# A table of steps for the work beside the output projection and the first two blocks of the MLP

## The chip, the cores and the metric

The kernel is one program on one core of one Trainium2 chip. TensorE (PE) does matrix products and transposes and writes to PSUM; VectorE (DVE) and ScalarE (ACT) do elementwise work, GpSimd (POOL) a little of it, SyncE (SP) and ACT issue transfers. Each engine runs its own queue in the order in which the program issued it, and waits at an instruction until what that instruction reads or overwrites is free. The metric is the time of one execution on the device, in microseconds, lower is better: 1658.2 is the median of 3 runs of the kernel before.

## The reference

One layer of a hybrid diffusion backbone on 1024 latent tokens and 128 context tokens (1152 rows, nine blocks t = 0..8 of 128) with 1024 channels. In float32:

```python
mod = (silu(cond) @ w_mod + b_mod)[:, None, :]
sh1, sc1, g1, sh2, sc2, g2 = split(mod, 6)
h = x * (1 + sc1) + sh1
q, k, v, u, bg, cg, ga, gc = split(h @ w_in, ...)
attn = merge_heads(attend(q, k, v)) @ w_attn_proj
conv = (bg * short_conv(cg * u, conv_w, conv_b)) @ w_conv_proj
mix = (sigmoid(ga) * attn + sigmoid(gc) * conv) @ w_o
x = layer_norm(ALPHA * x + g1 * mix, ln1_g, ln1_b)
h = x * (1 + sc2) + sh2
f = square(relu(h @ w1 + b1)) @ w2 + b2
x = layer_norm(ALPHA * x + g2 * f, ln2_g, ln2_b)
```

The case is about the stretch from `@ w_o` over the layer norm and `h = x * (1 + sc2) + sh2` to the beginning of `h @ w1`.

## The kernel before, in words

**Precision.** Every float32 operand is cut in a high part (a cast on ACT) and a low part (the rest, a subtraction on DVE), and a product is three matmuls: high by high, high by low, low by high.

**The output projection** has 18 units g = 0..17. A unit multiplies one block t of 128 tokens by one half (512) of the output channels: eight contraction steps kb of three matmuls (L1318, L1319, L1320), 24 in all, into one PSUM bank. The units run in three passes: half 0 of t0 to t5 (g0 to g5), half 1 of t0 to t8 (g6 to g14), half 0 of t6 to t8 (g15 to g17). In the last unit of a pass the weights of the next are split (L109 on ACT and L122 on DVE, L1257 and L1258 for some).

**Beside the projection.** After a unit, `ln1_sum` (L1047, L1048, L1051, all on DVE) adds the residual rows and takes statistics. Once both halves of a block are there, `ln1_apply` (with `moments`: DVE L1037, ACT's root L1038, DVE L1039 and L1040; then ACT L1059) normalizes the block. `turn` transposes a half of the block on PE (four transposes, L1113, to a bank) and writes it, scaled and shifted by the modulation, to the raw tiles, one column of 128 channels at a time, by ACT (L1126) or DVE (L1128). `n_vec` of the four columns are DVE's.

**The MLP's first layer** is a Winograd form of Strassen's scheme: 7 products instead of 8. The tokens are two pairs of 2 x 288 = 576 tokens. Pair 0 has t0 to t3 and the first half of t4, pair 1 the rest. Of a pair there are four raw tiles of 4 x 288 columns (`q00`, `q01`, `q10`, `q11`, holding B11, B12, B21, B22), with one buffer each, which both pairs use in turn. From them the sums T1 = B12 - B11, T3 = B22 - B12, T2 = B22 - T1 and T4 = B21 - T2 are made (`sub`, DVE L1151, over the raw tiles), and B11, T1, T2, B21, T3, B22, T4 are each cut in a high part (`high`, ACT L1140) and a low one (`low`, DVE L1147). A block multiplies one group of output channels by them in seven steps, in the order B11, B21, T1, T2, B22, T3, T4 (`ORDER`). The first two blocks are narrow: block 0 (steps 0 to 6) is for pair 0 alone and block 1 (steps 7 to 13) for pair 1 alone, so that block 0 can start before pair 1 is there. A step of theirs has 12 matmuls of 288 columns (L1388 to L1390), and after it ACT keeps the product (`keep`, L1451) or DVE adds it to a kept one (`plus`, L1454). All later blocks do both pairs; block 2's first product is written to a bank that the trace names dX. Weight sums (L826) and their splits (L1211 on ACT, L1212 on DVE) run some steps ahead, and ACT applies relu and square (L1396, L1397).

**What sets the order.** In the projection a queue `todo` holds pieces, each with a cost in microseconds that was written by hand; `spend(0.69)` after each kb of a unit adds credit and issues pieces from the front of the queue for as long as the credit is not negative. A unit's sum goes to the front, a turn to the end. In a pass's last unit nothing but one piece is issued. In the blocks, `beside` holds pieces by step of block 0, and `pair_parts(0..6)` issues the parts of pair 1 up to one step ahead of their use in block 1. The turns of t4 (second half), t5 and t6 for pair 1 are put at the queue's end and mostly run after the projection.

## Time and profile before

| | |
|---|---|
| median of 3 runs (lowest, highest) | 1658.2 us (1656.58, 1659.09) |
| the profiled execution: its time, its span | 1657.08 us, 1655.3 us |
| mean granted clock of PE in it | 0.986 |
| busy share of PE, DVE, ACT | 96%, 63%, 43% |
| projection and first two blocks in it, from g0 to the third block's first matmul | about 761.3 to 921.69 us |

A matmul's row in the trace begins where the previous one is well under way, so that the pitch of the starts and not the length of a row is what a matmul costs PE. Behind a row, in brackets, stands how long the engine had been idle and which instruction released it. In the table of waits a line reads: engine, tile and line of the waiting instruction, then what it waited for, then total, count and the longest in us. L numbers are lines of the kernel before; the changed kernel's lines are higher by some 5 to 40.

### The profile page before, as it was taken

What the parts mean: (1) busy time and instruction counts of PE and PEld (TensorE: products, weight loads), DVE (VectorE), ACT (ScalarE), POOL (GpSimd) and SP (SyncE); (2) the same over time, 40 slices, a digit from 0 to 9 for tenths busy, and PEclk for the clock granted to TensorE, in tenths of its full rate; (3) what the DMA queues carried; (4) which work ended last, traced back from release to release, by engine and by line L of the source; (5) the groups of instructions that cost most, each with busy time, mean ns of one, the idle gap of its engine ahead of it and who ended that gap; (6) DMA issues with size and microseconds to landing.
All of it is one profiled execution on the core that took longest, in us unless ns stands there. A gap on an engine that the chain in (4) does not pass through costs nothing.

```text
span 1655.3 us, 27274 instructions
## 1 busy us (share of the span) xinstructions
PE 1594.0 (96%) x10432; PEld 1536.8 (93%) x10432; DVE 1046.2 (63%) x1826; ACT 717.2 (43%) x1344; POOL 201.8 (12%) x214
## 2 busy tenths in 40 slices
PE   7999999999999999999988899999999999999995
PEld 5799999999999999998877899999999999999995
DVE  6568888665556553335577666666665558865666
ACT  5367777611112112222356556565565335453030
POOL 2145555100000002211000000000000121000002
PEclk9999999999999999999999999999999999999998
DMA  8432122142322323314333344554448898788792
GB/s 320 141 89 73 50 70 54 52 122 89 122 97 64 91 88 90 107 60 147 115 108 128 135 160 163 173 180 155 165 154 301 283 318 278 231 258 235 233 326 89
DMA packets 147563, 252.94 MB, mean 153 GB/s; under 512 B 40240, under 2 KB 58288, under 8 KB 147432
## 3 DMA queue, kind: packets, MB, share of 16 engines
q1 hardware_dynamic: 117064, 203.99, 39.0%
q10 hardware_dynamic: 30368, 47.20, 7.8%
q8 instruction: 82, 1.34, 0.3%
q14 instruction: 49, 0.40, 0.1%
HBM read 187.93 MB, written 63.21 MB: 152 GB/s over the span
## 4 chain that ended last, share of the span: by engine, by line
PE 79%; DVE 8%; ACT 5%; issue 3%; DMA 3%; POOL 1%; SPq 0%; POOLq 0%; ACTq 0%; DVEq 0%
PE ps L363 8%; PE ps L365 8%; PE ps L361 8%; PE pq L1641 6%; PE pq L1643 6%; PE pq L1642 6%; PE dX L1388 3%; PE dX L1390 3%; PE dX L1389 3%; PE dV L1388 2%; PE dV L1390 2%; PE dV L1389 2%; PE ps L882 2%; PE ps L883 2%; PE ps L881 2%
## 5 line engine op out<-in xcount | busy, mean ns | idle before, releaser
L365 PE MATMUL ps<-ahi,wl 128*128 128x384 f32 x864 | 292.6, 339 | 0.2 <-DVE wl L122 0.2
L363 PE MATMUL ps<-alo,wh 128*128 128x384 f32 x864 | 292.5, 338 | 0.0
L361 PE MATMUL ps<-ahi,wh 128*128 128x384 f32 x864 | 292.5, 338 | 0.0
L1641 PE MATMUL pq<-xh,vh 128*128 128x288 f32 x640 | 190.5, 298 | 4.7 <-ACT accc L1736 3.2
L1642 PE MATMUL pq<-xl,vh 128*128 128x288 f32 x640 | 189.6, 296 | 0.0
L1643 PE MATMUL pq<-xh,vl 128*128 128x288 f32 x640 | 189.0, 295 | 0.2 <-DVE vl L1631 0.2
L361 PEld LDWEIGHTS ps<-ahi,wh 128*128 128x128 f32 x864 | 162.4, 188 | 1.4 <-issue 0.2
L363 PEld LDWEIGHTS ps<-alo,wh 128*128 128x128 f32 x864 | 162.4, 188 | 0.7
L365 PEld LDWEIGHTS ps<-ahi,wl 128*128 128x128 f32 x864 | 162.4, 188 | 0.5 <-DVE wl L122 0.5
L1641 PEld LDWEIGHTS pq<-xh,vh 128*128 128x128 f32 x640 | 120.6, 188 | 5.6 <-ACT accc L1736 3.4
L1643 PEld LDWEIGHTS pq<-xh,vl 128*128 128x128 f32 x640 | 121.2, 189 | 0.4 <-DVE vl L1631 0.4
L1642 PEld LDWEIGHTS pq<-xl,vh 128*128 128x128 f32 x640 | 120.9, 189 | 0.1
L1608 DVE TENSOR_TENSOR xl<-hraw,xh 128x576 fp32r<-128x576 f32 x80 | 60.5, 756 | 74.5 <-ACT xh L1604 74.5
L122 DVE TENSOR_TENSOR wl<-wr,wh 128x1024 fp32r<-128x1024 f32 (+1 forms) x52 | 58.6, 1130 | 75.3 <-ACT wh L109 74.9
L1604 ACT CAST xh<-hraw 128x576 fp32r<-128x576 f32 x80 | 53.9, 673 | 96.4 <-issue 44.5
L1788 POOL TENSOR_TENSOR xm<-xm,ag 128x1024 f32<-128x1024 f32 x9 | 22.4, 2484 | 593.3 <-DMA w2r<-w 532.7
L743 DVE SCALAR_TENSOR_TENSOR acc<-wmb,sil,acc 128x512 f32<-128x512 f32 x112 | 78.2, 747 | 11.2 <-DMA wmb<-wmb 11.0
L109 ACT CAST wh<-wr 128x1024 fp32r<-128x1024 f32 (+1 forms) x60 | 55.9, 946 | 37.7 <-PE ps L1320 28.7
L563 ACT ACTIVATE s<-s,st 128x512 f32<-128x512 f32 (+1 forms) x72 | 49.6, 689 | 51.6 <-DVE st L561 51.1
L1451 ACT ACTIVATE c<-dX,b1c 128x576 f32<-128x576 f32 x45 | 33.3, 741 | 73.1 <-PE dX L1390 73.1
L882 PE MATMUL ps<-acl,wh 128*128 128x384 f32 x192 | 64.2, 334 | 0.0
L883 PE MATMUL ps<-ach,wl 128*128 128x384 f32 x192 | 64.2, 334 | 0.0
(378 smaller groups left out, 4388.6 us busy)
## 6 DMA issues: line engine op xcount, KB each, us to landing
w2r<-w SPq DMA_DIRECT2D x144, 256.0 KB
hraw<-hdT SPq DMA_DIRECT2D x60, 288.0 KB
wmb<-wmb SPq DMA_DIRECT2D x64, 256.0 KB
w1r<-w SPq DMA_DIRECT2D x30, 512.0 KB
hdB<-h ACTq DMA_DIRECT2D x48, 288.0 KB
hdT<-hT ACTq DMA_DIRECT2D x48, 288.0 KB
hraw<-hdB SPq DMA_DIRECT2D x44, 288.0 KB
mr<-wma SPq DMA_DIRECT2D x16, 512.0 KB
```

What stands on the lines that cost most here:

```text
L361: mm(b[:, :CH], lhsT=hi[:, ws], rhs=a[0][:, kb, :], start=first and kb == 0, stop=False)
L363: mm(b[:, :CH], lhsT=hi[:, ws], rhs=a[1][:, kb, :], start=False, stop=False)
L365: mm(b[:, :CH], lhsT=lo[:, ws], rhs=a[0][:, kb, :], start=False, stop=last and kb == n - 1)
L743: vec.scalar_tensor_tensor(out=a, in0=t, scalar=sil[:, k, cond:cond + 1], in1=a, op0=ALU.mult, op1=ALU.add)
L882: mm(b[:, :CH], lhsT=hi[:, ws], rhs=parts[kb][1][:, cs_], start=False, stop=False)
L883: mm(b[:, :CH], lhsT=lo[:, ws], rhs=parts[kb][0][:, cs_], start=False, stop=kb == 3)
L1388: mm(o, lhsT=hi[:, ws], rhs=xh, start=first and kb == 0, stop=False, **kw)
L1389: mm(o, lhsT=hi[:, ws], rhs=xl, start=False, stop=False, **kw)
L1390: mm(o, lhsT=lo[:, ws], rhs=xh, start=False, stop=kb == 3, **kw)
L1641: mm(o, lhsT=hi[:, ws], rhs=xh[:, i], start=j == 0, stop=False)
L1642: mm(o, lhsT=hi[:, ws], rhs=xl[:, i], start=False, stop=False)
L1643: mm(o, lhsT=lo[:, ws], rhs=xh[:, i], start=False, stop=j == NJ - 1)
```

## The change: what it does

1. *Projection by table.* The queue and its costs are gone. `at(g, kb, ...)` puts a piece into a slot of the table, after contraction step kb of unit g, and the loop issues what its slot holds. A unit's `ln1_sum` is issued after kb 0 of the next unit.
2. *Stages.* The layer norm is issued in two stages, `ln1_deviation` (statistics and root) after kb 1 and `ln1_apply` after kb 4; a turn in two stages, `across` (the transposes) and, one kb later, `modulated` (the columns).
3. *Columns.* Of a turn, half 0 goes to ACT whole and half 1 to DVE whole (t4's turn for pair 1: all on ACT), where before each half had columns of both.
4. *Tiles.* A raw tile is two tiles of 2 x 288 columns, so that sums and low parts are issued as two 576-wide instructions. The first raw tiles of pair 1 (B11, B21) have tiles of their own, taken from tiles that the blocks' sums use only later (`hT2`, `hT3`, `hT4`, `q`), and lie beside pair 0's. Its B12 and B22 use pair 0's. The residual rows of half 0 have six buffers instead of seven.
5. *Blocks by table.* `by(step, ...)` puts the pieces of pair 1 after the steps 0 to 10 of the first two blocks; the turns of t4, t5 and t6 for pair 1 are now in the projection (g13, g15, g17).

What PE multiplies is the same, in the same order but for the places of the transposes.

On DVE, from the last unit of the second pass (g14) to the weight splits of the third. `q_8188` is B11's raw tile, where T1 and then T2 are made, `q_8190` B21's; after the change `q_8194` and `q_8195` are the halves of B11's, `q_8196` and `q_8197` of B12's, `q_8200` and `q_8201` of B22's. Before:

```order
L1147 TENSOR_TENSOR hxahi_8410<-q_8188,hxahi_8280 128x576
L1147 TENSOR_TENSOR hxahi_8410<-q_8188,hxalo_8281 128x576
L1151 TENSOR_TENSOR q_8188<-q_8191,q_8188 128x1152
L1151 TENSOR_TENSOR q_8190<-q_8190,q_8188 128x1152
L1047 TENSOR_TENSOR lnt_8526<-ps_8478,g_7843 128x512
L1048 SCALAR_TENSOR_TENSOR xk_8285<-xk_8285,lnt_8526 128x512
L1051 BN_STATS bst_8529<-xk_8285 128x6
L122 TENSOR_TENSOR wl_8535<-wr_8066,wh_8534 128x1024
L122 TENSOR_TENSOR wl_8545<-wr_8080,wh_8544 128x1024
```

Now:

```order
L1187 TENSOR_TENSOR q_8196<-q_8200,q_8196 128x576
L1187 TENSOR_TENSOR q_8197<-q_8201,q_8197 128x576
L1183 TENSOR_TENSOR hxahi_8474<-q_8194,hxahi_8341 128x576
L1183 TENSOR_TENSOR hxahi_8474<-q_8195,hxalo_8342 128x576
L1053 TENSOR_TENSOR lnt_8556<-ps_8486,g_7843 128x512
L1054 SCALAR_TENSOR_TENSOR xk_8287<-xk_8287,lnt_8556 128x512
L1057 BN_STATS bst_8559<-xk_8287 128x6
L122 TENSOR_TENSOR wl_8565<-wr_8066,wh_8564 128x1024
L122 TENSOR_TENSOR wl_8575<-wr_8080,wh_8574 128x1024
```

The sums T2 and T4 (L1151) no longer stand ahead of the splits; the sum T3 (the first two rows now) does.

On DVE in block 1, from the sum T2 of pair 1 (`q_8711` before, `hT_8520` and `hT_8521` now) to T3's low part. `h_0_...` are the outputs of the block. Before:

```order
L1151 TENSOR_TENSOR q_8711<-q_8714,q_8711 128x1152
L1147 TENSOR_TENSOR hxs_9025<-q_8714,hxs_9024 128x1152
L1147 TENSOR_TENSOR hxs_9023<-q_8711,hxs_9022 128x1152
L1151 TENSOR_TENSOR q_8713<-q_8713,q_8711 128x1152
L1454 TENSOR_TENSOR h_0_8863<-ps_9068,c_0_8859 128x288
L1454 TENSOR_TENSOR h_0_8860<-ps_9096,c_0_8856 128x288
L1212 TENSOR_TENSOR w1wlo_9127<-w1r_0_8572,w1whi_9126 128x512
L826 TENSOR_TENSOR S_9143<-w1r_1_8573 128x512
L1212 TENSOR_TENSOR w1wlo_9127<-w1r_0_8572,w1whi_9126 128x512
L1147 TENSOR_TENSOR q_9066<-q_8713,hxs_9026 128x1152
```

Now, from T2's low part on:

```order
L1183 TENSOR_TENSOR hxs_9060<-hT_8520,hxs_9059 128x576
L1183 TENSOR_TENSOR hxs_9060<-hT_8521,hxs_9059 128x576
L1187 TENSOR_TENSOR hT_8522<-hT_8522,hT_8520 128x576
L1187 TENSOR_TENSOR q_8523<-q_8523,hT_8521 128x576
L1183 TENSOR_TENSOR q_9142<-hT_8522,hxs_9063 128x576
L1183 TENSOR_TENSOR q_9143<-q_8523,hxs_9063 128x576
L1236 TENSOR_TENSOR w1wlo_9169<-w1r_0_8602,w1whi_9168 128x512
L1183 TENSOR_TENSOR q_9160<-q_8756,hxs_9061 128x576
L1183 TENSOR_TENSOR q_9161<-q_8757,hxs_9061 128x576
L826 TENSOR_TENSOR S_9187<-w1r_1_8603 128x512
```

The low part of T4 (`q_9142`, `q_9143`) directly follows the sum T4, and only one weight's low part (L1236) is left ahead of T3's.

On ACT in the same place, `hxs_9022` is the high part of T2 before, `hxs_9026` that of T4, `q_9148` that of T3. Before:

```order
L1140 CAST hxs_9022<-q_8711 128x1152
L1140 CAST hxs_9026<-q_8713 128x1152
L1451 ACTIVATE c_0_8856<-ps_9082,b1c 128x288
L1451 ACTIVATE c_0_8857<-ps_9110,b1c 128x288
L1396 ACTIVATE h_0_8860<-h_0_8860 128x576
L1397 ACTIVATE h_0_8860<-h_0_8860 128x576
L1211 CAST w1whi_9126<-w1r_0_8572 128x512
L1451 ACTIVATE c_0_8858<-ps_9082,b1c 128x288
L1211 CAST w1whi_9126<-w1r_0_8572 128x512
L1140 CAST q_9148<-q_8712 128x1152
```

Now, with `hxs_9059` for T2, `hxs_9063` for T4 and `hxs_9061` for T3:

```order
L1179 CAST hxs_9059<-hT_8520 128x576
L1179 CAST hxs_9059<-hT_8521 128x576
L1179 CAST hxs_9063<-hT_8522 128x576
L1179 CAST hxs_9063<-q_8523 128x576
L1491 ACTIVATE c_0_8922<-ps_9146,b1c 128x288
L1179 CAST hxs_9061<-q_8756 128x576
L1179 CAST hxs_9061<-q_8757 128x576
L1432 ACTIVATE h_0_8925<-h_0_8925 128x576
L1433 ACTIVATE h_0_8925<-h_0_8925 128x576
L1235 CAST w1whi_9168<-w1r_0_8602 128x512
L1491 ACTIVATE c_0_8923<-ps_9104,b1c 128x288
```

T3's high part stood behind three kept products, the squares and two weight casts; now one kept product stands between T4's and T3's.

The diff, cut to its core:

```diff
 def load_xk(t, half):
-    xks[t, half] = tmp(xkp, [P, 512], f"xk{half}", 5 if half else 7)
+    xks[t, half] = tmp(xkp, [P, 512], f"xk{half}", 5 if half else 6)
...
+def raw_tiles(pair):
+    two = lambda k, x: [(raw_tile(k, x, i), 2 * i, 2) for i in range(2)]
+    if pair == 0:
+        return [[two(k, x) for x in range(2)] for k in range(2)]
+    first = [tmp(t1p, [P, 2, PT], t, 1) for t in ("hT2", "hT3", "hT4", "q")]
+    return [[[(first[2 * k], 0, 2), (first[2 * k + 1], 2, 2)], None] for k in range(2)]
...
-def turn(t, pair, half, n_vec=0):
-    def go():
+def turn(t, pair, half, on_vec):
+    b = []
+    def across():
+        b.append(turn_banks[0]())
+        turn_banks.rotate(-1)
         for i in range(4):
             nc.tensor.transpose(...)
+    def modulated():
...
-                if i < 4 - n_vec:
+                if not on_vec:
                     act(to_, from_, AF.Identity, scale=sc, bias=sh)
                 else:
                     vec.tensor_scalar(out=to_, in0=from_, ...)
-    return go
+    return across, modulated
...
+def at_turn(g, kb, t, pair, on_vec=True):
+    for half in range(2):
+        across, modulated = turn(t, pair, half, on_vec and half == 1)
+        at(g, kb, across)
+        at(g, kb + 1, modulated)
+for g, (ps, half, t) in enumerate(order):
+    if ps == 2 or ps == 1 and t < 6:
+        at(g + 1, 1, lambda t=t: ln1_deviation(t))
+        at(g + 1, 4, lambda t=t: ln1_apply(t))
+    if ps == 1 and t < 5:
+        at_turn(g + 2, 2, t, 0)
+at(12, 6, *parts0("sT1", "hT1"))
+at_turn(13, 2, 4, 1, on_vec=False)
+at(13, 4, *parts0("lT1", "hT3"))
+at(15, 1, *parts0("sT2", "hT2"))
...
-                if ps == 2 or t < ts_[-1]:
-                    spend(0.69)
+            if kb == 0 and waiting:
+                waiting()
...
+            for fn in slots.pop((g, kb), ()):
+                fn()
+        waiting = lambda t=t, half=half, b=b, x=gate_: ln1_sum(t, half, b, x, seen)
...
+by(8, *parts1("lT2", "sT4", "hT4"))
+by(9, *parts1("hT3", "lT4"))
+by(10, *parts1("lT3"))
...
-        while n == 1 and made <= min(i + 1, 6):
-            pair_parts(made)
...
+        for fn in beside.pop(s_, ()):
+            fn()
```

More of the change, by code (lines that the diff above doesn't have):

```diff
@@ L1091, in place @@
         for name in names:
-            own = ({"T4": (None, "q00"), "T3": ("q10", "q11")} if pair else {}).get(name, (None, None))
-            hx[pair][name] = tuple(x or next(store) for x in own)
+            low = {"B22": (0, 0), "T4": (1, 0), "T3": (1, 1)}.get(name) if pair else None
+            hx[pair][name] = next(store), low or next(store)
     def single(pool, n):
@@ new lines, in turn, with together, own @@
+        return across, modulated
+    def together(*pieces):
+        step = min(n for ops in pieces for _, _, n in ops)
+        for k in range(0, 4, step):
+            yield [next(ap[:, k - k0:k - k0 + step] for ap, k0, n in ops if k0 <= k < k0 + n) for ops in pieces]
+    def own(pair, name):
+        hx[pair][name] = tuple([(raw_tile(*x, i, F32R), 2 * i, 2) for i in range(2)] if isinstance(x[0], int) else x
+                               for x in hx[pair][name])
+        return hx[pair][name]
@@ new lines, in combine, with high, low @@
+    def combine(pair):
+        def high(name, x):
+            for h_, a in together(own(pair, name)[0], x):
+                nc.scalar.copy(h_, a)
+        def low(name, x):
+            for l_, a, h_ in together(own(pair, name)[1], x, hx[pair][name][0]):
+                vec.tensor_tensor(out=l_, in0=a, in1=f32(h_), op=ALU.subtract)
+        def sub(out, a, b):
+            for o_, a_, b_ in together(out, a, b):
+                vec.tensor_tensor(out=o_, in0=a_, in1=b_, op=ALU.subtract)
+        get = lambda name: raw[pair][("B11", "T1", "T2", "B12", "T3").count(name) == 0][name in ("B12", "T3", "B22")]
+        fns = {"sT1": lambda: sub(get("B11"), get("B12"), get("B11")), "sT3": lambda: sub(get("B12"), get("B22"), get("B12")),
+               "sT2": lambda: sub(get("B11"), get("B22"), get("B11")), "sT4": lambda: sub(get("T4"), get("T4"), get("B11"))}
+        for name in PARTS:
+            fns["h" + name] = lambda name=name: high(name, get(name))
+            fns["l" + name] = lambda name=name: low(name, get(name))
+        return lambda *names: [fns[name] for name in names]
@@ L1281, in emit @@
         next_xk()
-    seen, sums = {}, 0
-    todo = deque()
-    room = [0.0]
-    def spend(us):
-        room[0] = min(room[0] + us, 1.5)
-        while todo and (room[0] >= 0 or not todo[0][0]):
-            cost, fn = todo.popleft()
-            fn()
-            room[0] -= cost
-    turn_banks.extend(lambda i=i: bank(i) for i in range(4))
-    def put_turn(t, pair):
-        n_vec = 2 if not pair or t > 5 else 1
-        todo.extend((0.4 * n_vec, turn(t, pair, half, n_vec)) for half in range(2))
@@ new lines, in emit @@
+    at(10, 4, lambda: place0(0, ("B11", "B21")))
+    at(10, 6, *parts0("hB11"))
+    at(10, 7, *parts0("lB11", "hB21"))
+    at(11, 6, *parts0("lB21"))
+    at(12, 5, lambda: place0(1, ("T1", "T2", "T3", "B22", "T4"), [single(hx0, n) for n in range(4)]))
+    at(12, 6, *parts0("sT1", "hT1"))
+    at_turn(13, 2, 4, 1, on_vec=False)
+    at(13, 2, *parts0("sT3"))
+    at(13, 4, *parts0("lT1", "hT3"))
+    at(15, 1, *parts0("sT2", "hT2"))
+    at_turn(15, 3, 5, 1)
+    at(16, 1, *parts0("hB22"))
@@ L1358, in emit @@
+    waiting()
     sln.close()
@@ L1408, in emit @@
     after = late.append
-    made = 0
     def second_pair():
@@ L1442, in emit @@
             cs_ = [ht(t, n) for t in ("c1", "c5", "c2", "c3")]
[L1443 removed]
+            h = {m: ht("h" + m, n) for m in ("11", "22", "12", "21")}
         c1, c5, c2, c3 = (t[:, sl] for t in cs_)
@@ L1473, in finish, with sums @@
             late.append(lambda: parts("T4", h["T4"]))
-        def sums(h=h):
+        def sums(h=h, n=n):
+            for m in ("T2", "T3", "T4"):
+                h[m] = ht("h" + m, n)
             square(h["21"])
```

200 lines of the change are left out of this document (88 added, 112 removed).

## The prediction

> **What bounds the kernel now.** The page comes first: TensorE (PE) is busy for 96% of the span, so only its idle time and the time it spends at a lowered clock can be won without fewer matmuls, and the change has as many matmuls as before.
>
> ```profile
> span 1655.3 us, 27274 instructions
> PE 1594.0 (96%) x10432; PEld 1536.8 (93%) x10432; DVE 1046.2 (63%) x1826; ACT 717.2 (43%) x1344; POOL 201.8 (12%) x214
> ```
>
> Next come the waits between 740 and 930 us, which hold the whole region that the change touches (who waited for whom; total, times, longest, in us).
>
> ```profile
> PE ps L1318 <- ACT wh L109: 5.0, 2, 4.3
> PE ps L1388 <- ACT c L1451: 3.8, 2, 2.2
> PE ps L1388 <- ACT q L1140: 3.4, 1, 3.4
> PE ps L1319 <- DVE wl L122: 2.8, 2, 2.4
> PE ps L1388 <- DVE h L1454: 1.0, 1, 1.0
> PE ps L1113 <- ACT xk L1059: 1.0, 1, 1.0
> ...
> DVE q L1128 <- ACT q L1126: 15.4, 8, 2.8
> DVE bag L1039 <- ACT bag L1038: 3.4, 9, 0.4
> ```
>
> PE waits for weight splits (L109 on ACT, L122 on DVE) and, in the first two blocks, for kept products and for the B parts. Behind both stand ACT and DVE, which run the queued pieces in order. DVE itself stood 15.4 us in eight waits for ACT's columns of the same raw tile, and 3.4 us for the square root.
>
> The windows then say where it costs: from the start of g14 (848.10), the last unit of the second pass, to the first matmul of the third block (921.69), with the pieces inside. Columns: length, then busy time of PE, PE's weight load, DVE, ACT and POOL, then PE's granted clock, DMA share, GB/s.
>
> ```profile
> 810.56:816.98 6.42, 6.42 (x34) 5.29 (x33) 3.44 (x9) 3.20 (x7) 0.00 (x0) 1.00 0.26 89
> 842.59:848.10 5.51, 5.51 (x25) 4.50 (x24) 2.83 (x9) 2.99 (x7) 0.00 (x0) 1.00 0.24 89
> 853.60:858.06 4.46, 0.16 (x1) 0.00 (x0) 4.25 (x6) 3.30 (x4) 0.00 (x0) 0.92 0.00 0
> 858.06:864.18 6.12, 5.65 (x12) 4.10 (x13) 6.05 (x9) 2.98 (x5) 0.00 (x0) 0.50 0.50 170
> 877.98:921.69 43.71, 33.57 (x210) 31.94 (x209) 30.06 (x52) 27.29 (x56) 0.00 (x0) 0.85 0.27 96
> 848.10:921.69 73.59, 58.69 (x306) 51.58 (x305) 57.99 (x92) 40.67 (x74) 0.00 (x0) 0.86 0.31 104
> ```
>
> A unit of 24 matmuls is 5.51 us, one with a turn's eight transposes 6.42, so a turn costs PE 0.91 and a matmul of 512 columns 0.23. PE's own rows give the rest.
>
> ```profile
> 858.06 0.80 PE L1318 MATMUL ps<-wh,ahi 128*128 128x512 f32 x1 [4.30 <-ACT wh L109]
> ...
> 892.50 0.61 PE L1388 MATMUL ps<-hxs,w1whi 128*128 128x288 f32 x1 [2.18 <-ACT c L1451]
> ...
> 901.45 0.29 PE L1390 MATMUL ps<-hxahi,w1wlo 128*128 128x288 f32 x1
> ...
> 905.85 0.29 PE L1390 MATMUL ps<-hxalo,w1wlo 128*128 128x288 f32 x1
> ...
> 914.61 0.40 PE L1388 MATMUL ps<-q,w1whi 128*128 128x288 f32 x1 [3.36 <-ACT q L1140]
> ...
> 918.57 0.45 PE L1390 MATMUL ps<-q,w1wlo 128*128 128x288 f32 x1
> ...
> 921.69 0.45 PE L1388 MATMUL dX<-hxahi,w1whi 128*128 128x288 f32 x1
> ```
>
> From 901.45 to 905.85 lie 33 matmuls, 0.133 each; from 918.57 to 921.69 lie 13, 0.24 each, because after a hole the granted clock halves for a while. So the 73.59 us hold work for 49.0 at full clock: 4 units of 5.50 (22.0), 5 turns of 0.91 (4.6), 168 block matmuls of 0.133 (22.4). The other 24.6 are holes and half clock. Of these the step into the third pass has 7.8 (4.46 + 6.12 minus the 12 matmuls of 0.23) and the two blocks 16.7 (43.71 minus 22.4 and 4.6). That is all the change can win here.
>
> **The change, part by part.** *The step into the third pass.* Before, the pieces went out as their costs added up; DVE had the sums T1, T2 and T4 and the low part of T1 ahead of the weight splits, and came late. Now T2 goes to g15 and T4 to g17, and ahead of the splits stand T1, T3 and the low of T1. The other prices of DVE are these.
>
> ```profile
> 794.24 0.69 DVE L1047 TENSOR_TENSOR lnt<-ps,g 128x512 f32<-128x512 f32 x1 [3.36 <-PE ps L1320]
> ...
> 801.62 0.68 DVE L1047 TENSOR_TENSOR lnt<-ps,g 128x512 f32<-128x512 f32 x1
> ...
> 851.68 0.74 DVE L1147 TENSOR_TENSOR hxahi<-q,hxahi 128x576 fp32r<-128x576 f32 x1
> 852.34 0.75 DVE L1147 TENSOR_TENSOR hxahi<-q,hxalo 128x576 fp32r<-128x576 f32 x1
> ...
> 884.52 2.28 DVE L1128 TENSOR_SCALAR q<-ps,m2col 128x96 f32<-128x96 f32 x8 [0.78 <-ACT q L1126]
> ...
> 890.35 1.43 DVE L1128 TENSOR_SCALAR q<-ps,m2col 128x128 f32<-128x128 f32 x4 [2.28 <-PE ps L1113]
> ```
>
> A residual sum is three operations of 0.69, 2.1 us. A 576-wide pair is 1.32 us by its starts (852.34 minus 851.68, twice) or 1.49 by its durations; I take 1.4. In g10 to g13 I count 6.3, 5.5, 5.5 and 4.9 us of DVE work, 22.2, against 4 units of 6.42, 25.7: DVE keeps up, with 1 to 3 us to spare. The first pass boundary shows a DVE that is on time: from the last unit's residual sum to the end of all splits 7.4 us (794.24 to 801.62), and PE did not wait there beyond what its rows above show. So I price the boundary's loss at 0 and the gain at 7.8; bounds are 0 gained, if DVE is as late as before, and 7.8.
>
> *Columns of one half on one engine.* The 15.4 us of DVE waits for ACT were bought by sharing a tile. With half 0 on ACT and half 1 on DVE neither waits for the other within a turn, and for pair 0 ACT has four columns a turn as before. The cover is other DVE work; I count no separate gain, since the chain below is made of busy time.
>
> *The chain to the third block.* From the start of g14 DVE is the engine that the end hangs on, so I add it up: splits 7.6; four residual sums of 2.1 (8.4); five 576-pairs for pair 0 (7.0); columns 1.43 + 2.28 (3.7); small ones 1.2, some six of the form below. That is 27.9, while PE leaves the projection at 23.8 (4 units and two turns of 0.91). Then pair 1 up to its sum T4: ten pairs of 1.4 (14.0), two turns' columns (2.9), five additions of 0.45 (2.3), small ones 0.6: 19.8. DVE is then at 47.7.
>
> ```profile
> L1151 DVE TENSOR_TENSOR q<-q,q 128x1152 f32<-128x1152 f32 x8 | 10.8, 1354 | 0.1
> L1454 DVE TENSOR_TENSOR h<-ps,c 128x288 f32<-128x288 f32 x8 | 3.6, 453 | 3.4 <-ACT c L1451 3.3
> L1037 DVE BATCH_NORM_AGGREGATE bag<-bst 128x2 f32<-128x12 f32 x9 | 1.9, 208 | 0.3
> L1212 DVE TENSOR_TENSOR w1wlo<-w1r,w1whi 128x512 fp32r<-128x512 f32 x2 | 1.4, 689 | 2.0 <-ACT w1whi L1211 2.0
> ...
> L1140 ACT CAST hxahi<-q 128x576 fp32r<-128x576 f32 x2 | 1.4, 676 | 4.5 <-DVE q L1151 4.5
> L1451 ACT ACTIVATE c<-ps,b1c 128x288 f32<-128x288 f32 x8 | 3.9, 502 | 4.1 <-PE ps L1390 4.0
> L1396 ACT ACTIVATE h<-h 128x576 f32<-128x576 f32 x3 | 2.0, 681 | 0.1
> L1211 ACT CAST w1whi<-w1r 128x512 fp32r<-128x512 f32 x2 | 1.2, 607 | 0.0
> ```
>
> From there ACT's order counts, as the listing of its queue shows: high of T4 1.35 (two of 0.676), kept product c5 0.50, high of T3 1.35, two square operations 1.36, the weight cast 0.61, in sum 5.2, so 52.9; the low of that weight stands ahead of T3's low on DVE: 0.69 and a first piece of 0.75, so 54.3. PE then has two steps of 12 matmuls: 3.2 us at full clock, 5.8 at half. The third block starts 57.5 or 60.1 us after g14's start. Before it was 73.59, of which 0.9 is t4's turn, now ahead of g14: 72.7. The gain is 15.2 or 12.6; I take **14**, between them, because some hole before the last steps may reach 3 us, about the size of those that halved the clock.
>
> *Smaller tiles.* Pair 1's raw tiles no longer share pair 0's, so its first turns need not wait for pair 0's last low: this is what lets t4, t5 and t6 move into g13, g15 and g17. The price is 576-wide pieces for 1152-wide ones, some 15 pairs on DVE in this stretch: between 15 x (1.32 - 1.354), -0.5 us, and 15 x (1.49 - 1.354), +2.1; at 1.4 it is 0.7, already inside the chain. [...] Other edits (the split of the normalization in two, one buffer fewer for the residual rows) add no PE instruction and lie under units on which DVE is busy for about half (2.83 of 5.51); I cost them at 0. Without that cover the split's wait for the root, 0.4 a token block, would be won and not lost.
>
> **Rivals.** (a) *The clock stays full*: with holes of 1 to 3 us none fills the stretch after which it halved, so the steps take 3.2 and the gain is 15.2, about 1643 us. For it: the hole of 0.96 before 901.45's step left the rate at 0.133. Against: 0.95 and 2.18 us, close together, halved it. [...] (b) *DVE is late at the second boundary again*: by my count the transposes of t4 in g12 come some 0.1 us after its rows are normalized, and DVE's 22.2 of 25.7 leaves little; then 7.8 of loss stays there, DVE's later chain still gains: 1644 + 7.8, about 1652. (c) *The hole moves behind the blocks*: the weights' sums and casts, which DVE now does after T3, come 3 to 4 us late for the third block: 1648. (d) *It doesn't do what it says*: DVE's busy time, 57.99 of 73.59, is the bound and only its idle order changes; 1658. (e) *Slower*: the table fixes order, so ACT's kept product can queue behind a cast that waits for DVE's sum, which waits behind an addition that waits for the kept product. If every step of the 14 ran as such a chain, one cast pair (1.35), one low (1.4) and a step of matmuls (1.6) in row would take 4.35 a step, 60.9, and the third block would start 25.7 (23.8 and slack) + 60.9 = 86.6 after g14: 13.9 later, 1672. It decides from (72.7 - 25.7) / 14 = 3.36 us a step; before, a step took (43.71 - 4.6) / 14 = 2.8.
>
> **How the numbers follow.** The sum is made against the profiled execution, 1657.08 (span 1655.3); less 14 it is 1643.1, and the shown median is 1.1 above that execution, so **1644**. Chances: forecast 0.55 (its own range 1640.5 to 1648), (a) 0.15, (b) 0.12, (c) 0.08, (d) 0.04, (e) 0.06. The range from 1639.5 (both bounds of the pairs and the full clock) to 1652 leaves out (d), (e) and half of (b). About 0.2%, 3.3 us, is what a measurement can tell from no change. Faster by more: 0.55 + 0.15 + 0.12 + 0.08 = 0.90; same 0.04 (d); slower 0.06 (e).
>
> **What would show it.** In the profile after: no PE wait above 0.5 us for L109's or L122's successors at the step into the third pass, and clock 1.00 there; DVE's wait for ACT's columns under 3 us in sum; the stretch from g14's start to the first dX matmul 57 to 60 us; the last holes before T2, B22 and T3 under 3 us each, waiting for DVE's lows or a kept product. Wrong would be a stall at that step again, a block step longer than 3.36 us on average, or as many holes behind the first dX matmul as were lost ahead of it.

## The result, and the profile after

The changed kernel takes 1641.05 us (median of 4 runs, 1639.0 to 1644.34), the kernel before 1658.64 (4 runs, 1656.58 to 1659.64). The ratio is 0.9905 with a 95% interval of 0.9893 to 0.9917: it is about 1% faster, 17.6 us between the medians. Its profiled execution took 1641.01 us, 16.1 less than the one before.

The page of the changed kernel:

```profile
span 1639.2 us, 27293 instructions
PE 1587.7 (97%) x10432; PEld 1531.6 (93%) x10432; DVE 1045.2 (64%) x1845; ACT 718.0 (44%) x1356; POOL 201.8 (12%) x214
```

DVE and ACT are as busy as before (1046.2 and 717.2 us then), so nothing was taken off them; they only do it at other times. Next, who waited for whom from 725 to 925 us (total, times, longest, us), all rows of PE:

```profile
PE ps L1374 <- DVE wl L122: 2.4, 1, 2.4
...
PE ps L1425 <- DVE hxs L1183: 1.9, 1, 1.9
...
PE ps L1424 <- ACT c L1491: 1.6, 2, 1.1
...
PE ps L1373 <- ACT wh L109: 0.7, 1, 0.7
...
PE ps L1425 <- DVE q L1183: 0.6, 1, 0.6
...
PE ps L1424 <- ACT hxs L1179: 0.3, 1, 0.3
PE ps L1424 <- DVE h L1494: 0.2, 1, 0.2
```

The waits for weight splits (L1373, L1374) are those in the first pass, which were there before (L1318, L1319: the projection's matmuls lie 55 lines further down now, more than the 5 to 40 of the other lines). The one at the step into the third pass is gone, and no row is left in which DVE waits for ACT's columns (15.4 us before). The windows, with the columns of the prediction's table: g14, g15 to g17, the steps 0 to 9, the steps 10 to 13, a piece of step 10 and 11, and the whole from the start of g14 to the third block.

```profile
850.11:855.62 5.51, 5.51 (x25) 4.50 (x24) 4.77 (x6) 3.26 (x4) 0.00 (x0) 1.00 0.07 16
855.62:873.95 18.33, 18.33 (x90) 15.18 (x89) 17.93 (x40) 9.31 (x19) 0.00 (x0) 1.00 0.47 149
873.95:893.14 19.19, 18.56 (x137) 17.72 (x135) 17.29 (x35) 14.94 (x34) 0.00 (x0) 1.00 0.53 197
893.14:906.08 12.94, 8.78 (x48) 7.77 (x49) 10.28 (x17) 8.01 (x15) 0.00 (x0) 0.87 0.00 0
895.98:899.23 3.25, 2.76 (x12) 2.41 (x11) 2.87 (x5) 2.39 (x5) 0.00 (x0) 0.50 0.00 0
850.11:906.08 55.97, 51.18 (x297) 45.17 (x296) 50.27 (x95) 35.52 (x70) 0.00 (x0) 0.97 0.34 118
```

From g14 to the end of the projection PE is busy without a break now, at full clock, and DVE is busy for 17.93 of the 18.33 us of g15 to g17. From g14's start to the third block it is 55.97 us instead of 73.59. What is left of holes lies in steps 10 to 13, as PE's rows show:

```profile
893.14 0.40 PE L1424 MATMUL ps<-hxs,w1whi 128*128 128x288 f32 x1 [0.31 <-ACT hxs L1179]
895.48 0.40 PE L1425 MATMUL ps<-hxs,w1whi 128*128 128x288 f32 x1 [1.93 <-DVE hxs L1183]
...
898.59 0.61 PE L1424 MATMUL ps<-hxs,w1whi 128*128 128x288 f32 x1 [0.49 <-ACT c L1491]
...
901.93 0.40 PE L1424 MATMUL ps<-hxs,w1whi 128*128 128x288 f32 x1 [1.13 <-ACT c L1491]
902.93 0.40 PE L1425 MATMUL ps<-q,w1whi 128*128 128x288 f32 x1 [0.60 <-DVE q L1183]
...
906.08 0.29 PE L1424 MATMUL dX<-hxahi,w1whi 128*128 128x288 f32 x1
```

**A clean measure for the experiments.** The times of single executions of one kernel differ by up to 6.6 us, more than some parts of the change are worth. So each trace is also read by its *stretch*: from the first wait of the projection for its weights, which is in every trace, to the first dX matmul. That start moves by up to 1.5 us between traces for reasons ahead of the change. Of the kernel before and of the changed one it is this row:

```profile
764.92 0.51 PE L1318 MATMUL ps<-wh,ahi 128*128 128x512 f32 x1 [0.72 <-ACT wh L109]
```
```profile
766.01 0.50 PE L1373 MATMUL ps<-wh,ahi 128*128 128x512 f32 x1 [0.72 <-ACT wh L109]
```

The stretch was 921.69 - 764.92 = 156.77 us and is 906.08 - 766.01 = 140.07: 16.70 less. The changed execution came 1.09 us later to it and was 0.46 quicker behind it, which gives the 16.1 us of the two profiled executions. The table also parts the stretch at the first matmul of block 1 (901.09 before, 887.40 now).

The half clock moves these times by itself, at two places. In the first pass, behind a hole of about 2.37 us that all traces have, the next twelve matmuls took 4.07 to 4.45 us in twelve traces (a mean granted clock of 0.62 in the kernel before and in the changed one) and 2.89 and 2.90, or 0.24 us each, in two that kept the full clock there (T3 ahead; turns late and tiles shared): these two are 1.5 us shorter ahead of block 1 for a reason that no edit touches. In block 1, from the last hole to the first dX matmul, it is 3.15 to 3.18 us at full clock (changed, each tile shared, sums first, norm in one stage, turns late and tiles shared) and 4.43 to 5.69 where the clock halved (before 5.69, and the other three made from it; turns late 4.68; each bank shared 4.80). The granted clock of these stretches is 1.00 in the changed kernel and 0.50 in the kernel before. A difference of up to 2.5 us in the column of block 1 can thus be the clock's.

All runs in one table (time: median; ratio to the kernel before on the same chip, 95%):

| run | stretch, us | ahead of block 1 | block 1 | time, us | ratio |
|---|---|---|---|---|---|
| before | 156.77 | 136.17 | 20.60 | 1658.64 | |
| changed | 140.07 | 121.39 | 18.68 | 1641.05 | 0.9893 to 0.9917 |
| changed, each tile shared | 154.57 | 135.86 | 18.71 | 1655.1 | 0.9977 to 0.9996 |
| changed, each bank shared | 148.60 | 128.26 | 20.34 | 1648.35 | 0.9931 to 0.9961 |
| before, columns by half | 148.62 | 129.24 | 19.38 | 1650.38 | 0.9949 to 0.9973 |
| changed, sums first | 139.94 | 121.23 | 18.71 | 1644.43 | 0.9894 to 0.9930 |
| before, sums late | 154.43 | 134.11 | 20.32 | 1655.11 | 0.9973 to 0.9992 |
| before, columns by half and sums late | 148.32 | 128.68 | 19.64 | 1650.66 | 0.9942 to 0.9971 |
| changed, turns late | 144.22 | 124.01 | 20.21 | 1647.01 | 0.9921 to 0.9954 |
| changed, turns late and tiles shared | 141.90 | 123.98 | 17.92 | 1643.87 | 0.9899 to 0.9929 |
| changed, norm in one stage | 141.06 | 122.36 | 18.70 | 1641.65 | 0.9886 to 0.9915 |
| changed, T3 ahead | 136.50 | 120.21 | 16.29 | 1637.64 | 0.9869 to 0.9907 |
| changed, no filling work | 141.60 | 121.42 | 20.18 | 1642.51 | 0.9902 to 0.9932 |
| changed, T2 and T3 first | 135.23 | 121.42 | 13.81 | 1636.43 | 0.9854 to 0.9886 |

### The profile page after: what moved, and what is told of

Same layout as the page of the kernel before. It is cut to its first block, busy times and chain, and to the rows that moved or that the text cites. A ratio compares the mean times of both kernels' runs of the same rounds, so it can differ in the third digit from the quotient of the medians.

```text
span 1639.2 us, 27293 instructions
## 1 busy us (share of the span) xinstructions
PE 1587.7 (97%) x10432; PEld 1531.6 (93%) x10432; DVE 1045.2 (64%) x1845; ACT 718.0 (44%) x1356; POOL 201.8 (12%) x214
## 4 chain that ended last, share of the span: by engine, by line
PE 84%; DVE 6%; ACT 4%; issue 3%; DMA 3%; POOL 0%; SPq 0%; POOLq 0%; ACTq 0%; DVEq 0%
PE ps L363 8%; PE ps L365 8%; PE ps L361 8%; PE pq L1681 7%; PE pq L1683 6%; PE pq L1682 6%; PE dX L1424 3%; PE dX L1426 3%; PE dX L1425 3%; PE ps L1374 2%; PE ps L1375 2%; PE ps L1373 2%; PE dV L1424 2%; PE dV L1425 2%; PE dV L1426 2%
## 5 line engine op out<-in xcount | busy, mean ns | idle before, releaser
L530 POOL TENSOR_TENSOR bm<-E,mask 128x384 f32<-128x384 f32 x64 | 59.4, 929 | 38.7 <-DVE st L561 27.1
```

## The experiments

The theory of the prediction (1) was that the sums ahead of the weight splits made DVE and ACT late, and that DVE's busy time sets the rest. The rival (2) was that the two engines hand columns to each other and that both are late by that.

**Each tile shared.** ACT and DVE write a half's columns in turn.

```diff
-        across, modulated = turn(t, pair, half, on_vec and half == 1)
+        across, modulated = turn(t, pair, half, on_vec)
...
-                    if not on_vec:
+                    if not on_vec or i % 2 == 0:
```

> The changed kernel, but ACT and DVE share each raw tile again: of the four columns of a half ACT writes the first and third, DVE the second and fourth (t4's turn for pair 1 stays on ACT). Theory 1 (the sums that stood ahead of the weight splits made the step into the third pass slow; the waits for ACT's columns only add to DVE's chain): no hole at that step; DVE waits for ACT's columns again, 3 to 6 us behind g14, and the first dX matmul comes 56.0 + 1 to 4 us after g14's start, the time 1 to 4 us above the changed kernel's 1641. Theory 2 (the waits for the columns made DVE late at that step): a hole of 3 to 8 us at the step too, the time 5 to 11 us above 1641.

Measured: 1655.1 us and a stretch of 154.57, 14.5 longer: most of the gain is lost. Neither theory had it so: there is no hole at the step into the third pass, as theory 1 said, but the loss is above what theory 2 named. It is spread over what lies ahead of block 1: the transposes in g12 wait for rows that ACT normalizes too late, half clock follows them (eight matmuls of about 0.43 us instead of 0.23, from 844.20 to 847.56), and block 0 has six holes of 0.83 to 2.52 us, for weights, kept products, rows and an addition. Block 1 itself is as long as in the changed kernel.

```profile
842.48 1.36 PE L1143 MATMUL ps<-ident,xk 128*128 128x128 f32 x8 [2.63 <-ACT xk L1071]
```

The waits between the engines, from 800 to 922 us, where the kernel before shows the same 15.4 us in eight waits:

```profile
DVE q L1161 <- ACT q L1159: 14.9, 22, 1.9
ACT q L1159 <- DVE q L1161: 8.9, 15, 1.4
```

With alternate columns ACT waits for DVE too, which it did not before the change. So this run is harsher than the kernel before, and the next one is the fair one.

**Each bank shared.** The first two columns of a half on ACT, the last two on DVE, as before (there DVE had only one for t4 and t5 of pair 1); since the raw tile is cut in two, no raw tile is shared.

```diff
-        across, modulated = turn(t, pair, half, on_vec and half == 1)
+        across, modulated = turn(t, pair, half, on_vec)
...
-                    if not on_vec:
+                    if not on_vec or i < 2:
```

> The changed kernel, but of each half's four columns ACT writes the first two and DVE the last two, as before. With the cut tiles these lie in different raw tiles, but both engines read them from the one PSUM bank of that half's transposes, and the program still has DVE wait for ACT there. Theory 2a (what the two engines share is the bank, and sharing it delays both): DVE waits for ACT's columns 8 us or more in sum, time 1646 to 1655. Theory 2b (the raw tile is what they shared): those waits are under 3 us in sum and the time is within 2 us of 1641.

Measured: 1648.35 us, stretch 148.60, 8.53 longer than changed: 6.87 ahead of block 1, and in block 1 1.66 of half clock behind the last hole. Theory 2a: the waits are there although the tiles differ, 8.1 + 2.8 + 1.5 = 12.4 us.

```profile
DVE q L1161 <- ACT q L1159: 8.1, 6, 2.3
...
DVE hT L1161 <- ACT q L1159: 2.8, 1, 2.8
PE ps L1143 <- ACT xk L1071: 2.3, 2, 1.3
...
DVE hT L1161 <- ACT hT L1159: 1.5, 1, 1.5
```

In the second row DVE waits to write one tile until ACT is done with columns of another: what they have in common is the PSUM bank with the transposes. In the changed kernel, where one engine empties a bank, no such wait is left; whether the hardware needs the wait no run here shows.

**Columns by half, alone.** The kernel before, with only this part.

```diff
-                    if i < 4 - n_vec:
+                    if half == 0 or (t == 4 and pair):
```

> The kernel before, with one part of the change alone: half 0 of a turn goes to ACT whole and half 1 to DVE whole (t4 for pair 1 all to ACT); queue, costs, tiles, and stages as before. Theory 2 (the handover between the engines made both late): the waits of DVE for ACT's columns, 15.4 us, are gone, the hole at the step into the third pass is at most 2 us, and the kernel is 5 to 11 us faster than before. Rival (columns by half pay only together with the table): under 3 us faster.

Measured: 1650.38 us, 0.9949 to 0.9973, about 6.2 us under the 1656.53 of the kernel before beside it; stretch 148.62, 8.15 shorter. Theory 2 holds. Ahead of block 1, putting this part in alone (6.93) and taking it out alone (6.87) give the same; the rest of the 8.15 and 8.53 is half clock behind the last hole, shorter by 1.3 us here and longer by 1.7 there. The rows where PE waits, of this kernel:

```profile
854.10 0.49 PE L1318 MATMUL ps<-wh,ahi 128*128 128x512 f32 x1 [0.56 <-ACT wh L109]
...
855.36 0.50 PE L1319 MATMUL ps<-wl,ahi 128*128 128x512 f32 x1 [0.77 <-DVE wl L122]
...
893.89 0.40 PE L1388 MATMUL ps<-hxahi,w1whi 128*128 128x288 f32 x1 [3.51 <-DVE h L1454]
...
907.45 0.40 PE L1388 MATMUL ps<-q,w1whi 128*128 128x288 f32 x1 [3.36 <-ACT q L1140]
```

The hole at the step into the third pass fell from 4.30 + 0.46 to 0.56 + 0.77, although T2's and T4's sums still stand ahead of the splits. The hole in block 1 where T3's high comes late (907.45) is untouched, and ahead of block 1 PE now stands 3.51 us for an addition of DVE, where it was 0.96 before.

**Sums first.** The changed kernel with the order of before ahead of the splits.

```diff
-at(13, 2, *parts0("sT3"))
-at(13, 4, *parts0("lT1", "hT3"))
-at(15, 1, *parts0("sT2", "hT2"))
+at(13, 2, *parts0("hB22"))
+at(13, 4, *parts0("lT1"))
+at(13, 6, *parts0("sT2", "hT2", "sT4", "hT4"))
+at(15, 1, *parts0("sT3", "hT3"))
...
-at(16, 1, *parts0("hB22"))
...
-at(17, 7, *parts0("sT4", "hT4"))
```

> The changed kernel, but with the order of the kernel before ahead of the weight splits: B22's high, T1's low, the sums T2 and T4 and their highs stand in g13, T3's sum and high behind the splits in g15. Theory 1 (order of the sums): the hole and the half clock at the step into the third pass come back, 4.5 to 7.8 us, time about 1646 to 1649. Theory 2 (waits for columns): DVE has 1.6 us idle ahead of g13's residual sum and loses the sum T3 (1.3), which pays for the two sums (2.7): a hole under 0.5 us, time within 1.5 us of 1641.

Measured: a stretch of 139.94, against 140.07, and no wait of PE between the first pass and the blocks. Theory 2: the order of the sums decides nothing once the columns don't wait. The median, 1644.43, is 3.4 above the changed kernel's, outside the 1.5 us that theory 2 allowed, with overlapping intervals. In the profiled execution, 4.0 us longer, all of it lies behind the first dX matmul (737.9 us there against 733.1), far behind the edit; 1.9 us are a wait of PE at a line that both kernels share, the rest stays open.

**Sums late, alone, and with columns by half.** In the kernel before, T2, T4 and what follows go behind the splits; then both parts together.

```diff
+                def cut_in_two():
+                    pieces = combine(0)[1]
+                    todo.extendleft(reversed(pieces[:4]))
+                    behind.extend(pieces[4:])
+                behind = []
-                todo.append((0.0, lambda: todo.extendleft(reversed(combine(0)[1]))))
-                put_turn(4, 1)
-                put_turn(5, 1)
+                todo.append((0.0, cut_in_two))
+            if ps == 1 and t == 8:
+                todo.append((0.0, lambda: todo.extendleft(reversed(behind))))
+                put_turn(4, 1)
+                put_turn(5, 1)
```

> The kernel before, with one part of the change alone: the sums T2 and T4 and what follows them, and the turns behind those, are issued after the splits of the third pass. Theory 1: the hole of 4.46 us and the half clock behind it vanish; DVE has 2.7 us less ahead of the splits and ACT no cast that waits for a sum; 5 to 8 us faster than before, unless the blocks give it back (then the hole moves to block 0, and at least 3 us remain). Theory 2: DVE is late by its waits, more than 3 us of hole and half clock stay at the step, gain under 4 us.

> The kernel before with two parts of the change: columns by half, and the sums T2 and T4 behind the splits. Columns alone left holes of 0.56 and 0.77 us at the step into the third pass, sums late alone one of 2.34. If both act there, no hole is left, and the first dX matmul comes 1 to 2 us earlier than with columns alone, about 1649. If what the sums save only moves to the blocks, the time is that of columns alone, 1650.

Measured alone: 1655.11 us, 0.9973 to 0.9992, stretch 2.34 shorter. A hole of 2.34 us stays at the step, now for DVE's split alone:

```profile
857.04 0.50 PE L1319 MATMUL ps<-wl,ahi 128*128 128x512 f32 x1 [2.34 <-DVE wl L122]
```

That is theory 2's "under 4 us". The half clock that follows (eight matmuls of about 0.43 us instead of 0.23, from 858.34 to 861.72) adds about 1.5 us, so that more than 3 us of hole and half clock stay at the step, as theory 2 said. Together with columns by half: the hole at the step is gone, as expected, but the stretch is 148.32 against 148.62 with columns alone, and the time the same. What the sums save moves on to the blocks, but for 0.56 us ahead of block 1: theory 1's 7.8 us for the order of the sums falls.

**Turns late, and tiles shared.** The changed kernel with the turns of t4 to t6 for pair 1 after step 0; then also with the raw tiles of both pairs shared and T3 and T4 placed as before.

```diff
-at_turn(13, 2, 4, 1, on_vec=False)
-at_turn(15, 3, 5, 1)
-at_turn(17, 3, 6, 1)
+turns = [turn(t, 1, half, t > 4 and half == 1) for t in (4, 5, 6) for half in range(2)]
+by(0, lambda: ln1_deviation(8), *[f for x in range(0, 6, 2) for y in (0, 1) for f in (turns[x][y], turns[x + 1][y])])
```
```diff
-low = {"B22": (0, 0), "T4": (1, 0), "T3": (1, 1)}.get(name) if pair else None
+hi, low = ({"T4": (None, (0, 0)), "T3": ((1, 0), (1, 1))}.get(name, (None, None)) if pair else (None, None))
...
-        if pair == 0:
+        if pair in (0, 1):
...
-by(9, *parts1("hT3", "lT4"))
-by(10, *parts1("lT3"))
+by(9, *parts1("lT4"))
+by(10, *parts1("hT3", "lT3"))
```

> The changed kernel, but the turns of t4, t5 and t6 for pair 1 are issued behind the projection, after step 0 of block 0, as they mostly were before; raw tiles and all else stay. Theory 1 (DVE's busy time is the chain, it does the same work in another order): first dX matmul 0 to 1.5 us later, time 1641 to 1643. Rival (the places of the turns give the gain in the blocks): the columns pile up in block 0, the raw tiles of pair 1 are whole 3 us or more later, time 1644 to 1648.

> The run with the turns of t4 to t6 behind the projection, and in addition pair 1's first raw tiles share pair 0's buffers as before (T4's low in B11's tile, T3's high and low in B21's and B22's, so T3's high comes behind T4's low; pair 0's T4 low is issued ahead of pair 1's first turn). Theory (own tiles pay for themselves, by letting T3's high run early): the hole of about 3.4 us ahead of step 12 is back, the first dX matmul 2 to 5 us later than with the turns late alone, time 1648 to 1651. Rival (own tiles are worth nothing but for the earlier turns): within 1.5 us of that run's 1647.

Measured: turns late 1647.01 us, stretch 144.22, 4.15 longer than changed. Ahead of block 1 it is 2.62 longer. The rival is right here: the places of the turns matter, since ACT's columns pile up behind the projection, where the next transposes wait for the bank, and DVE's busy time is not the whole chain:

```profile
874.93 0.33 PE L1143 MATMUL ps<-ident,xk 128*128 128x128 f32 x1 [0.72 <-ACT hT L1159]
...
877.52 1.09 PE L1143 MATMUL ps<-ident,xk 128*128 128x128 f32 x8 [0.74 <-ACT hT L1159]
```

The other 1.53 us are half clock in the last two steps, behind a hole of the same length as in the changed kernel, 4.68 us from here to the first dX matmul instead of 3.15:

```profile
904.99 0.40 PE L1422 MATMUL ps<-q,w1whi 128*128 128x288 f32 x1 [0.60 <-DVE q L1183]
...
909.67 0.29 PE L1421 MATMUL dX<-hxahi,w1whi 128*128 128x288 f32 x1
```

With the tiles shared as well it is 1643.87 and 141.90, that is 2.3 us *shorter*, against both expectations. Some 1.5 of the 2.3 is the clock: this trace has no half clock in the first pass and in the last two steps, 1.5 us each, but one in block 0 (matmuls 0.24 us apart from 878.39 to 879.59), where it takes 16.06 us from the first waiting transposes (873.80) to block 1 instead of 14.53. The rest, 0.8 us, is won ahead of step 12: the hole of 3.4 us did not come back, and PE stood 0.90 us for T3's high and 0.39 for its low, instead of 1.49 for a kept product and 0.60 for the low. So tiles of their own gave nothing here but the early turns, and both together are worth about 2.6 us ahead of block 1. That run also issues the last low of pair 0 earlier, and this was not tried apart.

**Norm in one stage.**

```diff
-at(g + 1, 1, lambda t=t: ln1_deviation(t))
-at(g + 1, 4, lambda t=t: ln1_apply(t))
+at(g + 1, 4, lambda t=t: (ln1_deviation(t), ln1_apply(t)))
```

> The changed kernel with the layer norm in one stage: statistics, root and apply are issued together after kb 4. DVE waits for the root again, 0.4 us in each of nine blocks. If only that is lost, the first dX matmul comes 0 to 2 us later and the time is 1641 to 1643. Rival (the stages are what keeps ACT's normalization ahead of the transposes): transposes wait for normalized rows, 1 us or more each, 3 us or more in sum, 1644 or above.

Measured: 1641.65 us, stretch 141.06, 0.99 longer, all of it ahead of block 1: within the first expectation. The wait for the root is back, and the stretch grows by about a third of it:

```profile
DVE bag L1045 <- ACT bag L1042: 3.6, 9, 0.4
```

**The last four steps in another order.** The trace of the changed kernel shows how steps 10 to 13 are lost. ACT and DVE there:

```profile
896.84 0.67 ACT L1179 CAST hxs<-hT 128x576 fp32r<-128x576 f32 x1 [3.08 <-DVE hT L1187]
897.46 0.67 ACT L1179 CAST hxs<-q 128x576 fp32r<-128x576 f32 x1
898.04 0.50 ACT L1491 ACTIVATE c<-ps,b1c 128x288 f32<-128x288 f32 x1
...
900.88 0.60 ACT L1235 CAST w1whi<-w1r 128x512 fp32r<-128x512 f32 x1
901.39 0.49 ACT L1491 ACTIVATE c<-ps,b1c 128x288 f32<-128x288 f32 x1
```
```profile
896.68 0.75 DVE L1187 TENSOR_TENSOR q<-q,hT 128x576 f32<-128x576 f32 x1
...
901.51 0.69 DVE L1236 TENSOR_TENSOR w1wlo<-w1r,w1whi 128x512 fp32r<-128x512 f32 x1 [2.55 <-ACT w1whi L1235]
902.12 1.42 DVE L1183 TENSOR_TENSOR q<-q,hxs 128x576 fp32r<-128x576 f32 x2
```

ACT stands 3.08 us for T4's sum with the kept product of step 9 (898.04) behind it, for which step 11 waits; DVE then stands 2.55 us for a weight's cast with T3's low (902.12) behind it, for which step 12 waits. Three orders were tried:

```diff
-by(8, *parts1("lT2", "sT4", "hT4"))
-by(9, *parts1("hT3", "lT4"))
-by(10, *parts1("lT3"))
+by(8, *parts1("lT2", "sT4"))
+by(9, *parts1("hT3", "lT3", "hT4", "lT4"))
```

> The changed kernel with the end of block 1 in another order: the high of T4 after the kept product of step 9 and behind the high of T3, and T3's low ahead of T4's and ahead of the first weight's low. In the changed kernel ACT stood 3.1 us before T4's high with the kept product behind it, and T3's low stood behind a weight's low that waited 2.5 us for ACT. If the holes of 0.49, 1.13 and 0.60 us ahead of steps 11 and 12 come from that order, they vanish: first dX matmul 2 to 3.4 us earlier, 1638 to 1639. If DVE's busy time sets the end anyway, they move to step 13 and under 1 us is gained.

Measured: 1637.64 us, stretch 3.57 shorter. In block 1 it is 2.39 shorter, as expected; 1.5 us are the first pass at full clock, which the edit does not touch. The first reading holds for two of the three holes (0.49, 0.60); the third, for the kept product of step 10, is still there with 1.61 us. By its time alone this run is not told apart from the changed kernel: their intervals overlap.

```diff
-by(5, *parts1("sT1", "hT1", "sT3"))
-by(6, *parts1("hB22", "lT1"))
-by(7, *parts1("sT2", "hT2", "lB22"))
-...
+by(5, *parts1("sT1", "hT1"))
+by(6, *parts1("lT1", "sT2", "hT2"))
+by(7, *parts1("lT2", "hB22", "lB22", "sT3"))
+by(8, *parts1("hT3", "lT3", "sT4"))
+by(9, *parts1("hT4", "lT4"))
```

> As the run with T3 ahead, and B22's parts and the sum T3 no longer stand between T1's sum and T2's low on DVE. T2's low comes 2 to 2.7 us earlier, so the hole of 1.93 us ahead of step 10 and the half clock behind it vanish as well; DVE is then the bound up to T4's low and a hole of about 1 us each stays ahead of steps 12 and 13. First dX matmul 3 to 4.5 us earlier than in the changed kernel, 1636.5 to 1638. If what is saved at step 10 returns whole at steps 12 and 13, it equals the run with T3 ahead.

Measured: 1642.51 us, stretch 1.53 *longer* than changed: a miss. The hole of 1.93 us in step 10 did go (0.43 is left ahead of it), but a kept product now stood on ACT behind casts that were asked for early, and PE waited 2.67 and 1.54 us for kept products. The holes of steps 10 to 13 sum to 4.64 us, against 4.46 in the changed kernel: what was saved came back whole, and ACT's order, not DVE's, was the bound there. The loss itself is the clock's: the last two steps took 5.38 us (902.21 to 907.59; the matmuls are 0.24 us apart up to 906.69, and 0.133 from 906.92 on).

```diff
+by(7, *parts1("sT2", "hT2"))
+by(8, *parts1("lT2", "lB22"))
+by(9, *parts1("hT3", "lT3", "sT4"))
+by(10, *parts1("hT4", "lT4"), lambda: w1_prep(14))
...
-            w1_prep(s_ + 4)
+            if s_ != 10:
+                w1_prep(s_ + 4)
...
-            do_late()
+            if s_ != 9:
+                do_late()
```

> The run with T3 ahead, further: T2's low directly behind T2's sum and ahead of B22's low, T3's low ahead of T4's sum, and on ACT step 10's kept product ahead of T4's high, the squares and the first weight cast of block 2. Against that run, whose holes were 1.94 us (T2's low) and 1.61 us (the kept product): the second goes, of the first at most 0.8 stays, small holes of under 0.5 us come ahead of steps 11 and 13, and the clock stays full; first dX matmul 1.5 to 2.7 us earlier, about 1635.5. If it is DVE's busy time that sets T4's low, under 0.7 us is gained.

Measured: 1636.43 us, 0.9854 to 0.9886, stretch 135.23, 4.84 shorter than changed, all of it in block 1, and 1.27 shorter than with T3 ahead. In block 1, where that run's full clock in the first pass plays no part, it is 2.48 shorter, as expected. It is below both kernels, and its interval does not touch the changed kernel's. PE's rows from step 10 on:

```profile
893.85 0.40 PE L1425 MATMUL ps<-hxs,w1whi 128*128 128x288 f32 x1 [0.60 <-DVE hxs L1183]
...
899.36 0.40 PE L1425 MATMUL ps<-q,hiB 128*128 128x288 f32 x1 [0.39 <-DVE q L1183]
...
900.91 0.29 PE L1424 MATMUL dX<-hxahi,w1whi 128*128 128x288 f32 x1
```

## Why the prediction was right, point by point

The forecast was 1644 with a range of 1639.5 to 1652, and faster; measured were 1641.05. The direction and the region are right, the size was forecast 2.7 us small in the stretch, and one of its causes was wrong. The lower end of the range does not follow from the terms named for it: the full clock gives 1643, and pairs of 1.32 instead of 1.4 take off another 1.2, so 1641.8, and the measured time lies just below that.

**The step into the third pass.** The stall of 7.8 us went whole, as forecast. But *the step that named its cause failed*: "DVE had the sums T1, T2 and T4 and the low part of T1 ahead of the weight splits, and came late". Moving the sums alone gave 2.34 us, moving them back cost nothing, and columns by half alone, with the sums where they were, cut the hole to 0.56 + 0.77.

**Columns of one half on one engine.** "I count no separate gain" is the worst term: it is the largest part of the change, 6.9 us of the 16.70 ahead of block 1, put in alone or taken out. Nor are the waits "bought by sharing a tile": with separate tiles 12.4 us of them stay as long as both engines empty one bank, and none is left in the changed kernel, where a bank has one engine. That the sum came out nevertheless is in part luck: the chain was made of busy times, which is how DVE runs only without these waits, so the gain was counted under other names.

**The chain to the third block.** DVE was forecast to finish T4's sum 47.7 us after g14's start; it did at 896.68 + 0.75 - 850.11 = 47.3. Two errors cancel in that: DVE waited 0.87 and 0.90 us ahead of two additions in block 0, which the chain had at nothing, and its pairs were shorter than 1.4. ACT's tail from there to the end of the weight cast was forecast at 5.2 us and took 900.88 + 0.60 - 897.43 = 4.1: the mis-sized term, since ACT casts the first half of T4 while DVE still makes the second (896.84, against 897.43), and rows that follow each other start closer than their lengths (the two halves 0.62 us apart at 0.67 each). The two last DVE pieces and PE's two steps were as forecast, the latter at full clock (902.93 to 906.08, granted clock 1.00, 3.15 us against 3.2). That the clock was full there is luck as far as the traces show: behind the same hole of 0.60 us it halved with the turns late (4.68 us). So the third block started after 55.97 us and not 57.5, and the gain is 73.59 - 0.91 - 55.97 = 16.7, against 15.2 at full clock and 14 taken between the clocks.

**Smaller tiles.** A pair of 576 takes 1.33 us by its starts in the new trace, below the 1.4 taken, and an instruction of 1152 took 1.27 (866.05 to 867.32 in the kernel before), so the cut costs 0.06 to 0.07 us a pair, about 1 us for fifteen, against 0.7 forecast (whose upper bound, 15 x (1.49 - 1.354), is 2.0 and not 2.1). That the tiles of their own allow the early turns is right; the turns' places are worth 2.6 us by themselves, which the chain of busy time did not tell.

**The edits costed at 0.** The norm's two stages are worth 0.99 us of stretch, not 0. (No filling work and T2 and T3 first, whose edits hardly touch what lies ahead of block 1, differ there from the changed kernel by 0.03.)

**The rivals.** (a) The clock was full in the last two steps, where the sum needed it; it did halve once in steps 10 and 11, at no cost that shows (last section). (b) DVE was not late at the second boundary; the small margin of t4's transposes in g12 was real, as they waited 2.63 us with each tile shared and 1.33 at the longest with each bank shared. (c) No hole moved behind the blocks: from the first dX matmul to the end it is 733.1 us, 733.6 before. (d) fell. (e) The steps of the two blocks take (906.08 - 873.95 - 1.82) / 14 = 2.2 us each with two turns taken off, far from 3.36; but its mechanism, a kept product behind a cast that waits for a sum, is what is left in steps 10 to 13, and what the run without filling work ran into.

**Not divided.** Of the 16.70 us 14.78 lie ahead of block 1. Of these, columns by half are 6.9, the early turns and the tiles that allow them 2.6, the norm's stages 1.0, the order of the sums between 0 and 0.6 once the columns do not wait. What remains, about 4, was not tried alone. Most of it can be seen at block 1's first matmul, which waits for an addition of DVE. In the kernel before with columns by half and sums late, that addition stands behind pair 1's sums T1 and T3 and T1's low, and PE stands 3.52 us:

```profile
890.17 2.75 DVE L1151 TENSOR_TENSOR q<-q,q 128x1152 f32<-128x1152 f32 x2
...
894.29 0.46 DVE L1461 TENSOR_TENSOR h<-ps,c 128x288 f32<-128x288 f32 x1
```
```profile
894.80 0.40 PE L1395 MATMUL ps<-hxahi,w1whi 128*128 128x288 f32 x1 [3.52 <-DVE h L1461]
```

In the changed kernel the addition is issued ahead of these sums, and PE stands 0.21 us:

```profile
886.88 0.46 DVE L1494 TENSOR_TENSOR h<-ps,c 128x288 f32<-128x288 f32 x1 [0.90 <-ACT c L1491]
887.26 1.42 DVE L1187 TENSOR_TENSOR hT<-q,hT 128x576 f32<-128x576 f32 x2
```
```profile
887.40 0.40 PE L1424 MATMUL ps<-hxahi,w1whi 128*128 128x288 f32 x1 [0.21 <-DVE h L1494]
```

That this order is the cause is argued from the rows, not tried. Block 1 itself is only 1.92 us shorter, and the full clock of its last two steps alone is 2.54 (5.69 us before, 3.15 now). So that T3's high no longer stands behind squares and weight casts won nothing that shows: the holes of 3.36 and 0.99 us ahead of step 12 shrank to 1.13 and 0.60, but from block 1's first matmul to step 12 it is 14.53 us now and was 13.52.

## What to carry to other kernels

Where two engines emptied one PSUM bank between them, DVE waited 12.4 us for ACT's columns here, and for none where each bank had one engine (the changed kernel); so try a whole bank for one engine and the next bank for the other before moving any work. A wait between two engines that are off the critical path can be the cause of a stall of the engine on the path that names something else, so test such waits first: here DVE, 63% busy, stood 15.4 us for columns, and with these waits gone PE's hole for a weight split fell from 4.30 us to 0.56. Put what the critical engine waits for ahead of a cast whose input is not yet there, and see what each wait has behind it in its queue: here ACT stood 3.08 us for T4's sum with a kept product behind it, and PE then 0.49 us for that product.
